# Dilated mixer: merge factors one visit later, merge two visits later, held-back output projection spread over the last visit's turns

## The chip, the core and the metric

One Trainium2 chip, one core of it. The metric is the device time of one execution in microseconds (us); the median of three runs counts. An engine is named as in the profile: PE is TensorE (matmuls), PEld its weight loads, DVE is VectorE, ACT ScalarE, POOL GpSimd and SP SyncE. SP issues the weight loads, ACT and POOL issue other DMAs.

## The reference

An encoder of two post-norm layers on 512 tokens of width 1024. Layer 0 mixes tokens by differential attention, layer 1 by dilated attention; each layer then attends into 256 memory tokens and applies a gated MLP with a convolution. Each sub-layer is `x <- LayerNorm(ALPHA * x + sublayer(x))`. The change lies in layer 1's mixer: three groups of dilated window attention, merged by their softmax denominators:

```python
qkv = (x @ w_qkv).reshape(B, S, G, 3, H, E)
for g, (window, dilation) in enumerate(((128, 1), (512, 4), (2048, 16))):
    o, l = dilated_group(qkv[:, :, g, 0], qkv[:, :, g, 1], qkv[:, :, g, 2], window, dilation, slopes)
    outs.append(o); lses.append(l)
wts = jax.nn.softmax(jnp.stack(lses), axis=0)
o = jnp.sum(wts[..., None] * jnp.stack(outs), axis=0)
return o.reshape(B, S, D) @ w_o
```

## The kernel before

All matmuls of weights are done in three passes (`mm3`, L239 to L241): an operand is split into a high and a low part (`whi`, `wlo`), and high times high, high times low and low times high are summed. SP loads a unit of weights of 512 KB into `raw` (four buffers), ACT casts the high part (L218), DVE subtracts for the low part (L219); there are six buffers for each part, and a cast waits until PE has finished with the unit that held its buffer.

The order of PE's instructions is the order in which the code issues them (`tc.manual_schedule(engines={PE})`). DVE, ACT, POOL and SP get theirs from the framework's scheduler, which plans with estimates of its own and may put an instruction ahead of one that the code issues earlier. Each engine then executes strictly in that order.

The dilated mixer (`dil_attention`) treats 16 heads as eight pairs p, and each pair in two halves v. `main` makes one visit i for each half (p = i // 2, v = i % 2), and one visit more. In visit i:

- `scores(p, v)`: 24 matmuls (L716) into four banks `S`; then for each bank and group the minimum and the bias on DVE (L725, writes `u` and the statistics `st`) and the exponential on ACT (L727). `u` has four buffers, so a bank's softmax waits for the transposes of the same bank of the visit before.
- four turns: `turn(u, n)` transposes one `u` of the visit before into a bank `t` of pool `pt`, which has two (L770), and copies it to SBUF as `PT`: DVE for n = 0 and 2, ACT for 1 and 3 (L772).
- `values` of the visit before (L785), copied into the tiles `O` (L789 to L793).

At the end of `scores(p, 1)` the code calls `factors(p)`: the statistics go to DRAM (three DMAs, `sd`) and come back in another order (`x`), all issued by POOL; DVE and ACT work out the weights of the merge (L750 to L759); they go to DRAM (`fd`) and come back broadcast as `F` (L764). At the end of `values(p, 1)` DVE merges: L795 to L797, then `evac` splits the result into `o1h` (ACT) and `o1l` (DVE), the input of the output projection.

`weave` fills the gaps in PE's order: with the next pair's projections (`proj`), and in the last three visits with the output projection of token block q = 0 (`on_.early(0)`, 12 `mm3` into `ps_a`) for the units u = 0 to 2, which use only pairs 0 to 5. The same for q = 1 is held back (`late`, 12 `mm3` into banks `S`) and taken in the last visit.

After the mixer, `OutNorm.finish` loads gain and bias of the norm (two DMAs on ACT's queue, L366, 512 KB each) and the residual rows of the four token blocks (four DMAs there, L371, 512 KB each). It computes what needs no pair 6 or 7 of blocks 2 and 3 (`first`), then the rest block by block; unit (u, hf) is the u-th of four weight units of output half hf, and unit 3 needs pairs 6 and 7. Each block is normed (`norm`: L414, L417 on DVE; L418 on ACT; L421, L422 on DVE; a power on POOL, L423; L426 on DVE), and transposed for the next sub-layer (`turn` of `OutNorm`, L432) when PE's planned time has passed a due time. The first keys of the cross-attention (`mem_keys`) are filled in behind.

Of the kernel before, what the change touches and what calls it, by code (L numbers as in the profile page):

```python
# [9 lines left out]
F32 = mybir.dt.float32  # L10
# [7 lines left out]
SEQ = 512  # L18
# [129 lines left out]
def encoder(ctx: ExitStack, tc: tile.TileContext, wall, xin, lam, subln, conv, lngb, tabf, tabd, eye, out):  # L148
# [497 lines left out]
    def dil_attention(act, oT, pools, vp, ap, on_, led):  # L646
        tab = vp.tile([128, 768], F32, name="tabd")
        nc.scalar.dma_start(tab, tabd)
        NP = LH // 2
        qk, v0, v12, st0, st12, O = {}, {}, {}, {}, {}, {}  # L650


        def keys(x, b):
# [50 lines left out]
        def scores(p, v):  # L704
            (q0, k0, q1, k1, q2, k2) = qk[p]
            if v == 0:
                st0[p] = ap.tile([128, 4, 4], F32, tag="st0", name="st0")
                st12[p] = ap.tile([128, 4, 4], F32, tag="st12", name="st12")
            bs = 2 * v, 2 * v + 1
            Ss = {(b, c): psS.tile([128, 512], F32, tag="s", name="S") for b in bs for c in range(2)}  # L710
            for b in bs:
                for q_, k_, f in ((q0, keys(k0, b), slice(0, 256)), (q1, k1[:, b, :], slice(256, 384)),
                                  (q2, k2[:, b, :], slice(384, 512))):
                    for c in range(2):
                        h = sl(c, 64)
                        nc.tensor.matmul(Ss[b, c][:, f], q_[h, b, :], k_[h], start=True, stop=True)  # L716
            us = []
            for (b, c), S in Ss.items():
                u = ap.tile([128, 512], F32, tag="u", name="u", bufs=4)
                slope = 2.0 ** (-(2 * p + c + 1) / 2.0)  # L720
                for n, s in enumerate((st0[p], st12[p])):
                    f = sl(n, 256)
                    t = tab[:, 512:768] if n else tab[:, sl(b // 3, 256)]
                    m = s[:, b, 2 * c:2 * c + 1]
                    nc.vector.tensor_tensor_reduce(out=u[:, f], in0=S[:, f], in1=t, scale=-slope,  # L725
                                                   scalar=3.0e38, op0=ALU.add, op1=ALU.min, accum_out=m)
                    nc.scalar.activation(u[:, f], u[:, f], AF.Exp, bias=m, scale=-1.0,  # L727
                                         accum_out=s[:, b, 2 * c + 1:2 * c + 2])
                us.append(u)
            if v == 1:  # L730
                O[p] = [ap.tile([128, 512], F32, tag=f"O{n}", name="O", bufs=1) for n in range(2)], factors(p)
            return us

        def factors(p):

            eng = nc.gpsimd
            sd = dram.tile([SEQ, 4], F32, name=f"sd{p}")
            fd = dram.tile([2, 2, SEQ], F32, name=f"fd{p}")
            a, b = st0.pop(p), st12.pop(p)
            eng.dma_start(sd[64:448, :].rearrange("(b p) k -> p b k", p=128), a[:, 0:3, :])  # L740
            eng.dma_start(sd[448:512, :], a[0:64, 3, :])
            eng.dma_start(sd[0:64, :], a[64:128, 3, :])
            x = ap.tile([128, 4, 4], F32, tag="x0", name="x0")
            eng.dma_start(x, sd.rearrange("(k r) c -> k r c", r=4))

            ms = [t.rearrange("p r (c k) -> p k c r", k=2) for t in (x, b)]
            w = ap.tile([128, 2, 2, 4], F32, tag="w0", name="w0")
# [14 lines left out]
            for c in range(2):  # L762
                f = fd[c]
                eng.dma_start(F[sl(c, 64)], bass.AP(f.tensor, f.offset, [[0, 64], [SEQ, 2], [1, SEQ]]))  # L764
            return F

        def turn(u, n):
            tp = bank(pt, "t").rearrange("p (a b) -> p a b", b=128)
# [6 lines left out]
        def values(p, v, PTs):  # L775
            o = bank(pt, "t")
            for x in range(2):
                b = 2 * v + x
                for n in range(4):
                    for c in range(2):  # L780
                        if n < 2:
                            V = v0[p // 2][b + n if b < 3 else 3 * n][:, (p % 2) * 128 + c * 64:]
                        else:
                            V = v12[p // 2][b][:, (p % 2) * 256 + (n - 2) * 128 + c * 64:]
                        nc.tensor.matmul(o[sl(c, 64), sl(2 * (n // 2) + x)], V[:, :64], PTs[2 * x + c][:, n, :],  # L785
                                         start=n % 2 == 0, stop=n % 2 == 1)
            (o0, o12), F = O[p]
            if v == 0:
                nc.scalar.copy(o0[:, 64:320], o[:, 0:256])  # L789
            else:  # L790
                nc.scalar.copy(o0[:, 320:512], o[:, 0:192])
                nc.scalar.copy(o0[:, 0:64], o[:, 192:256])
            nc.vector.tensor_copy(classes(o12)[:, sl(v, 2), :], o[:, 256:512].rearrange("p (r k) -> p r k", r=2))  # L793
            if v == 1:
                nc.vector.tensor_tensor(o0, o0, F[:, 0], op=ALU.mult)  # L795
                nc.vector.tensor_tensor(o12, o12, F[:, 1], op=ALU.mult)
                nc.vector.tensor_tensor(o0, o0, o12, op=ALU.add)  # L797
                evac(o0, oT[0][:, p, :], oT[1][:, p, :])

        def two_banks():  # L800
            return [psS.tile([128, 512], F32, tag="s", name="S") for _ in range(2)]
# [3 lines left out]
        def main():  # L805
            n = 2 * NP
            us = {}
            for i in range(n + 1):
                seg, step = (i // 2, 1 / 2.0) if i < n - 2 else (NP - 1, 1 / 3.0)
                pos = seg + (i - 2 * seg) * step  # L810
                yield pos
                if i < n:
                    us[i] = scores(i // 2, i % 2)
                else:
                    take(late, 1300)
                if i > 0:
                    PTs = []
                    for k in range(4):
                        yield pos + (TURN0 + TURNS * k) * step
                        PTs.append(turn(us[i - 1][k], k))  # L820
                    yield pos + VALUES * step
                    if i == n:
                        take(late, 1300)
                    values((i - 1) // 2, (i - 1) % 2, PTs)

        run(proj(0))
        weave(main(), [(proj(p + 1), 6 * 5184 + 31104 * (p % 2)) for p in range(NP - 1)]
# [124 lines left out]
    for l in range(2):  # L952
# [4 lines left out]
        with ExitStack() as cz:  # L957
# [20 lines left out]
            else:  # L978
                with ExitStack() as cp:
# [5 lines left out]
                    with ExitStack() as c:  # L985
# [2 lines left out]
                        two, pt = dil_attention(act, oT, pools, vp, ap, on, led)  # L988
                    kv = memory()
                    act, res, _ = on.finish(lambda q: two() if q == 2 else [bank(pt, "t") for _ in range(2)],  # L990
                                            [(((0, 0), (1, 0)), (2, 3))], res, False,
                                            lambda q: two if q else (pa, "a"),
                                            lambda a: mem_keys(mt_kv["mt"], kv, range(3)))
                pz = cz.enter_context(others("pz1"))
# [67 lines left out]
```

## Time and profile before

| | |
|---|---|
| three runs | 1899.86, 1897.64, 1900.0 us; median 1899.86 |
| profiled execution | 1899.72 us, of it 1897.9 us span |
| granted TensorE clock, mean | 0.998 |
| busy: PE, PEld, DVE, ACT, POOL | 1871.9, 1574.6, 952.9, 763.3, 73.0 us |
| visits of the dilated mixer | from 874.8 (first L716) to 1323 us |
| its output projection and norm | from 1323 to 1369.6 us (last L432) |

The profile lists, for each engine, the time it sat idle before an instruction and what ended that wait. `PE ps_t L770 <- DVE PT L772: 5.3, 2, 4.4` means that PE stood 5.3 us in two waits ahead of the transposes of line 770, the longest 4.4, until DVE's copy of line 772 had ended. A row of a timeline gives start, duration, engine, line, operation, output and input, count, and in brackets the wait ahead. Waits on PE cost time; waits on the others do so only if PE then waits for them.

### The profile page before, as it was taken

The numbers are of one execution on the slowest core, as the hardware profiler recorded it, in microseconds if no ns is written. First come the engines' busy times: TensorE is split into PE (matmuls) and PEld (weight loads), VectorE is DVE, ScalarE is ACT, GpSimd is POOL, SyncE is SP. The second block draws the span as 40 slices with busy tenths as digits, with TensorE's granted clock in tenths as the row PEclk, the third lists the DMA queues.
The fourth block names the chain that finished last, engine by engine and source line by source line (L and its number), as shares of the span: only waits on it lengthen the run. The fifth ranks groups of instructions, "written<-read, shape, count | busy, mean of one in ns | idle before, by whom it ended". The sixth has DMA issues, their size and how long they took to land.

```text
span 1897.9 us, 25004 instructions
## 1 busy us (share of the span) xinstructions
PE 1871.9 (99%) x9896; PEld 1574.6 (83%) x9896; DVE 952.9 (50%) x1761; ACT 763.3 (40%) x1372; POOL 73.0 (4%) x116
## 2 busy tenths in 40 slices
PE   9999999999999999999999999998999999999998
PEld 7777788889888888898898898987888898888886
DVE  5588675557444432533444344444855564444324
ACT  4567654325333321324434344343544243333211
POOL 0001110000000000000000000001000000000000
PEclk9999999999999999999999999999999999999999
DMA  6121066234332334332322232221651352333241
GB/s 237 45 78 56 23 219 191 67 118 150 100 97 93 100 100 151 104 120 100 97 77 84 78 101 87 80 80 46 224 189 65 122 157 90 99 100 96 93 144 45
DMA packets 61573, 204.35 MB, mean 108 GB/s; under 512 B 8080, under 2 KB 8720, under 8 KB 61456
## 3 DMA queue, kind: packets, MB, share of 16 engines
q1 hardware_dynamic: 46080, 165.89, 27.5%
q10 hardware_dynamic: 12816, 32.47, 4.7%
q0 software_dynamic: 2560, 4.39, 1.0%
q8 instruction: 78, 1.28, 0.3%
q14 instruction: 39, 0.32, 0.1%
HBM read 190.01 MB, written 12.71 MB: 107 GB/s over the span
## 4 chain that ended last, share of the span: by engine, by line
PE 92%; DVE 4%; DMA 2%; ACT 1%; issue 1%; POOL 0%; DVEq 0%; POOLq 0%; ACTq 0%; SPq 0%
PE ps_a L239 17%; PE ps_a L240 16%; PE ps_a L241 16%; PE ps_o L239 7%; PE ps_o L241 7%; PE ps_o L240 7%; PE ps_s L241 2%; PE ps_s L240 2%; PE ps_s L239 2%; PE ps_t L239 2%; PE ps_t L241 2%; PE ps_t L240 2%; PE S L716 1%; PE ps_t L785 1%; PE ps_t L770 1%; PE ps_o L582 1%
## 5 line engine op out<-in xcount | busy, mean ns | idle before, releaser
L219 DVE TENSOR_TENSOR wlo<-raw,whi 128x1024 fp32r<-128x1024 f32 (+1 forms) x309 | 376.7, 1220 | 454.5 <-ACT whi L218 449.3
L218 ACT CAST whi<-raw 128x1024 fp32r<-128x1024 f32 (+1 forms) x309 | 323.6, 1049 | 574.3 <-PE ps_a L240 277.6
L239 PE MATMUL ps_a<-x2h,whi 128*128 128x512 f32 (+1 forms) x384 | 152.4, 397 | 0.0
L241 PE MATMUL ps_a<-x2h,wlo 128*128 128x512 f32 (+1 forms) x384 | 146.6, 382 | 0.0
L240 PE MATMUL ps_a<-x2l,whi 128*128 128x512 f32 (+1 forms) x384 | 146.2, 381 | 0.0
L239 PE MATMUL ps_a<-whi,x2h 128*128 128x512 f32 (+1 forms) x256 | 90.2, 352 | 0.0
L725 DVE CUSTOM_DVE_ANT_0 u<-S,tabd 128x256 f32<-128x256 f32 x128 | 48.8, 420 | 79.0 <-PE ps_t L770 78.2
L240 PE MATMUL ps_a<-wlo,x2h 128*128 128x512 f32 (+1 forms) x256 | 87.1, 340 | 0.0
L241 PE MATMUL ps_a<-whi,x2l 128*128 128x512 f32 (+1 forms) x256 | 87.1, 340 | 0.0
L241 PEld LDWEIGHTS ps_a<-x2h,wlo 128*128 128x128 f32 x384 | 72.2, 188 | 14.5
L239 PEld LDWEIGHTS ps_a<-x2h,whi 128*128 128x128 f32 x384 | 72.3, 188 | 14.3 <-issue 1.5
L727 ACT ACTIVATE u<-u,st 128x256 f32<-128x256 f32 x128 | 64.0, 502 | 47.2 <-DVE st L725 47.0
L240 PEld LDWEIGHTS ps_a<-x2l,whi 128*128 128x128 f32 x384 | 72.5, 189 | 11.6
L239 PE MATMUL ps_o<-x1h,whi 128*128 128x512 f32 (+1 forms) x192 | 71.6, 373 | 0.0
L239 PE MATMUL ps_o<-x4h,whi 128*128 128x512 f32 (+1 forms) x192 | 71.6, 373 | 0.0
L240 PE MATMUL ps_a<-x4l,whi 128*128 128x512 f32 (+1 forms) x192 | 71.3, 372 | 0.0
L239 PE MATMUL ps_a<-x1h,whi 128*128 128x512 f32 (+1 forms) x192 | 71.3, 372 | 0.0
L240 PE MATMUL ps_a<-x1l,whi 128*128 128x512 f32 (+1 forms) x192 | 71.3, 372 | 0.0
L239 PE MATMUL ps_a<-x4h,whi 128*128 128x512 f32 (+1 forms) x192 | 71.3, 371 | 0.0
L241 PE MATMUL ps_a<-x4h,wlo 128*128 128x512 f32 (+1 forms) x192 | 71.3, 371 | 0.0
L241 PE MATMUL ps_a<-x1h,wlo 128*128 128x512 f32 (+1 forms) x192 | 71.3, 371 | 0.0
L241 PE MATMUL ps_o<-x1h,wlo 128*128 128x512 f32 (+1 forms) x192 | 71.3, 371 | 0.0
(420 smaller groups left out, 4487.5 us busy)
## 6 DMA issues: line engine op xcount, KB each, us to landing
raw<-in_wall_dram SPq DMA_DIRECT2D x314, 512.0 KB, 3.5
y<-row ACTq DMA_DIRECT2D x40, 256.0 KB, 3.0
row<-y ACTq DMA_DIRECT2D x20, 512.0 KB, 5.4
row<-in_lngb_dram ACTq DMA_DIRECT2D x12, 512.0 KB, 4.6
F<-fd POOLq DMA_DIRECT2D x16, 256.0 KB, 4.3
row<-in_x_dram ACTq DMA_DIRECT2D x4, 512.0 KB, 6.5
out_dram<-row ACTq DMA_DIRECT2D x8, 256.0 KB, 2.1
raw<-in_wall_dram ACTq DMA_DIRECT2D x2, 256.0 KB, 4.4
```

Of the source, the lines that this page charges most:

```text
L218: nc.scalar.copy(hi, ps)
L219: nc.vector.tensor_tensor(lo, ps, hi.bitcast(F32), op=ALU.subtract)
L239: nc.tensor.matmul(ps, ah, bh, start=start, stop=False)
L240: nc.tensor.matmul(ps, ah, bl, start=False, stop=False)
L241: nc.tensor.matmul(ps, al, bh, start=False, stop=stop)
L582: nc.tensor.matmul(o, PT[:, k, :], V[:, k, sl(h)], start=k == 0, stop=k == 3)
L716: nc.tensor.matmul(Ss[b, c][:, f], q_[h, b, :], k_[h], start=True, stop=True)
L725: nc.vector.tensor_tensor_reduce(out=u[:, f], in0=S[:, f], in1=t, scale=-slope, scalar=3.0e38, op0=ALU.add, op1=ALU.min, accum_out=m)
L727: nc.scalar.activation(u[:, f], u[:, f], AF.Exp, bias=m, scale=-1.0, accum_out=s[:, b, 2 * c + 1:2 * c + 2])
L770: nc.tensor.transpose(tp[:, k, :], u[:, sl(k)], ident)
L785: nc.tensor.matmul(o[sl(c, 64), sl(2 * (n // 2) + x)], V[:, :64], PTs[2 * x + c][:, n, :], start=n % 2 == 0, stop=n % 2 == 1)
```

## The change

`factors` is cut in two. Its DMAs to `sd` and back to `x` become `exchange(p)`, called where `factors` was, at the end of `scores(p, 1)`. The rest stays `factors(p)` and is called one visit later, after the four turns and ahead of `values`. The merge leaves `values` and becomes `merge(p)`, called in the second visit after `scores(p, 1)`, behind its second turn; the last pair's after the loop. In the last visit the held-back projection is taken three `mm3` at a time ahead of each of the four turns, where three stood ahead of the turns, three ahead of `values` and six after it. In `finish`, unit (2, 0) joins `first`, so blocks 2 and 3 compute four `mm3` more ahead of the first unit that needs pairs 6 and 7.

```diff
@@ scores @@
             if v == 1:
-                O[p] = [ap.tile([128, 512], F32, tag=f"O{n}", name="O", bufs=1) for n in range(2)], factors(p)
+                exchange(p)
             return us
-        def factors(p):
+        def exchange(p):
...
             x = ap.tile([128, 4, 4], F32, tag="x0", name="x0")
             eng.dma_start(x, sd.rearrange("(k r) c -> k r c", r=4))
+            X[p] = x
+
+        def factors(p):
+            eng = nc.gpsimd
+            fd = dram.tile([2, 2, SEQ], F32, name=f"fd{p}")
+            x, b = X.pop(p), st12.pop(p)
...
-            return F
+            Fs[p] = F
@@ values @@
-            (o0, o12), F = O[p]
+            if v == 0:
+                O[p] = [ap.tile([128, 512], F32, tag=f"O{n}", name="O", bufs=1) for n in range(2)]
+            o0, o12 = O[p]
...
-            if v == 1:
-                nc.vector.tensor_tensor(o0, o0, F[:, 0], op=ALU.mult)
-                nc.vector.tensor_tensor(o12, o12, F[:, 1], op=ALU.mult)
-                nc.vector.tensor_tensor(o0, o0, o12, op=ALU.add)
-                evac(o0, oT[0][:, p, :], oT[1][:, p, :])
+
+        def merge(p):
+            (o0, o12), F = O.pop(p), Fs.pop(p)
+            nc.vector.tensor_tensor(o0, o0, F[:, 0], op=ALU.mult)
+            nc.vector.tensor_tensor(o12, o12, F[:, 1], op=ALU.mult)
+            nc.vector.tensor_tensor(o0, o0, o12, op=ALU.add)
+            evac(o0, oT[0][:, p, :], oT[1][:, p, :])
@@ main @@
-                else:
-                    take(late, 1300)
                 if i > 0:
                     PTs = []
                     for k in range(4):
                         yield pos + (TURN0 + TURNS * k) * step
+                        if i == n:
+                            take(late, (1900, 1300)[k > 0])
                         PTs.append(turn(us[i - 1][k], k))
+                        if k == 1 and i % 2 and i > 1:
+                            merge((i - 3) // 2)
+                    if i % 2 == 0:
+                        factors((i - 2) // 2)
                     yield pos + VALUES * step
                     if i == n:
                         take(late, 1300)
                     values((i - 1) // 2, (i - 1) % 2, PTs)
+            merge(NP - 1)
@@ finish of the dilated mixer @@
-                                            [(((0, 0), (1, 0)), (2, 3))], res, False,
+                                            [(((0, 0), (1, 0), (2, 0)), (2, 3))], res, False,
```

What the scheduler makes of it is seen in the order of the built programs. DVE, in visit 14, where pair 6's factors meet the softmax (L725) and the first turn's copy of that visit; `w` are the factors, `x` what came back from DRAM. Before:

```order
L793 COPY O<-ps_t 128x2x128
L750 TENSOR_TENSOR w_10608<-x_10604,st_10368 128x8
L752 TENSOR_TENSOR w_10606<-w_10608,x_10604 128x2x4
...
L757 RECIPROCAL w_10608<-w_10608 128x8
L759 TENSOR_TENSOR w_10606<-w_10607,w_10608 128x2x4 x2
L725 ISA u,st_10754<-S,tabd 128x256
...
L772 COPY PT<-ps_t 128x512
```

And DVE at the same place in the changed program (L756 is the old L750, L778 the old L772):

```order
L801 COPY O<-ps_t 128x2x128
L756 TENSOR_TENSOR w_10831<-x_10596,st_10350 128x8
L758 TENSOR_TENSOR w_10829<-w_10831,x_10596 128x2x4
...
L763 RECIPROCAL w_10831<-w_10831 128x8
L765 TENSOR_TENSOR w_10829<-w_10830,w_10831 128x2x4 x2
L725 ISA u,st_10736<-S,tabd 128x256
...
L778 COPY PT<-ps_t 128x512
```

Nothing moved: though the code now issues the factors after visit 14's softmax and turns, the scheduler puts them ahead of both, as it did before. The same holds for every merge up to pair 6 and for ACT and POOL: up to visit 15 the four orders are the same row for row, but for line numbers and buffer names.

PE, in the last visit, from the first turn on; `S` is the held-back projection of block 1, `ps_a` that of block 0. Before:

```order
L770 MATMUL ps_t<-ident,u 128x128 x4
L239 MATMUL ps_a<-whi_10796,o1h 128x512
L240 MATMUL ps_a<-wlo_10797,o1h 128x512
L241 MATMUL ps_a<-whi_10796,o1l 128x512
L770 MATMUL ps_t<-ident,u 128x128 x4
L239 MATMUL ps_a<-whi_10822,o1h 128x512
```

And PE there in the changed program:

```order
L776 MATMUL ps_t<-ident,u 128x128 x4
L239 MATMUL ps_a<-whi_10778,o1h 128x512
L240 MATMUL ps_a<-wlo_10779,o1h 128x512
L241 MATMUL ps_a<-whi_10778,o1l 128x512
L239 MATMUL S<-whi_10523,o1h 128x512
L240 MATMUL S<-wlo_10524,o1h 128x512
...
L776 MATMUL ps_t<-ident,u 128x128 x4
```

Three `mm3` of block 1 now stand between two turns; as many fewer stand after the values.

ACT, at the start of `finish`: the cast of the last pair's merged output (`o1h`), the casts of the units (3, 0) and (3, 1) and the DMAs of gain and bias (L366) and of the residual rows (L371). Before:

```order
L218 CAST o1h<-O 128x512
L366 DMA row_11124<-in_lngb_dram 128x1024
L218 CAST whi_10935<-raw_10933 128x1024
L366 DMA row_11125<-in_lngb_dram 128x1024
L218 CAST whi_10961<-raw_10959 128x1024
L371 DMA row_11128<-y_5882 128x1024
```

And ACT there in the changed program:

```order
L218 CAST whi_10910<-raw_10908 128x1024
L218 CAST o1h<-O 128x512
L218 CAST whi_10941<-raw_10939 128x1024
L366 DMA row_11124<-in_lngb_dram 128x1024
L366 DMA row_11125<-in_lngb_dram 128x1024
L371 DMA row_11128<-y_5882 128x1024
```

Both casts of weights now stand ahead of the two DMAs of gain and bias, and these stand directly ahead of the residual rows.

More of the change, by code (lines that the diff above doesn't have):

```diff
@@ L649, in dil_attention @@
         NP = LH // 2
-        qk, v0, v12, st0, st12, O = {}, {}, {}, {}, {}, {}
+        qk, v0, v12, st0, st12, O, X, Fs = {}, {}, {}, {}, {}, {}, {}, {}
         def keys(x, b):
@@ L730, in scores @@
             if v == 1:
-                O[p] = [ap.tile([128, 512], F32, tag=f"O{n}", name="O", bufs=1) for n in range(2)], factors(p)
+                exchange(p)
             return us
-        def factors(p):
+        def exchange(p):
             eng = nc.gpsimd
             sd = dram.tile([SEQ, 4], F32, name=f"sd{p}")
-            fd = dram.tile([2, 2, SEQ], F32, name=f"fd{p}")
-            a, b = st0.pop(p), st12.pop(p)
+            a = st0.pop(p)
             eng.dma_start(sd[64:448, :].rearrange("(b p) k -> p b k", p=128), a[:, 0:3, :])
```

## The prediction

> **What bounds the kernel now.** I read the page first, then PE's waits, then the timelines of the engines around each wait. The page's head:
>
> ```profile
> span 1897.9 us, 25004 instructions
> PE 1871.9 (99%) x9896; PEld 1574.6 (83%) x9896; DVE 952.9 (50%) x1761; ACT 763.3 (40%) x1372; POOL 73.0 (4%) x116
> ```
>
> PE is idle for 26 us in all, so only PE's waits can be won. The waits from 1256 to 1350 us, the end of the mixer:
>
> ```profile
> PE ps_t L770 <- DVE PT L772: 5.3, 2, 4.4
> PE ps_a L432 <- DVE row L426: 2.1, 1, 2.1
> PE ps_t L785 <- DVE PT L772: 0.4, 1, 0.4
> ```
>
> From 860 to 1256 us, the visits 0 to 12, the same view is empty: there the factors and merges hold up nobody, and moving them is worth nothing. Two places remain. The first is visit 14 (PE, then DVE):
>
> ```profile
> 1296.00 0.63 PE L770 MATMUL ps_t<-ident,u 128*128 128x128 f32 x4 [4.37 <-DVE PT L772]
> ...
> 1307.31 0.63 PE L770 MATMUL ps_t<-ident,u 128*128 128x128 f32 x4 [0.92 <-DVE PT L772]
> ...
> 1309.50 1.97 PE L785 MATMUL ps_t<-PT,V 128*64 128x128 f32 x32 [0.43 <-DVE PT L772]
> ```
>
> ```profile
> 1292.86 0.17 DVE L750 TENSOR_TENSOR w<-x,st 128x8 f32<-128x8 f32 x1 [5.22 <-DMA x<-sd]
> ...
> 1295.17 0.68 DVE L772 COPY PT<-ps_t 128x512 f32<-128x512 f32 x1
> ...
> 1302.42 0.69 DVE L795 TENSOR_TENSOR O<-O,F 128x512 f32<-128x512 f32 x1
> ...
> 1306.47 0.69 DVE L772 COPY PT<-ps_t 128x512 f32<-128x512 f32 x1
> ```
>
> DVE stands 5.22 us at the factors of pair 6 until the statistics are back from DRAM. Behind them in its queue are the softmax and the copy that frees a bank for PE's third transpose; PE waits 4.37 us. One visit on, DVE merges pair 6 ahead of the softmax and the copy; PE waits 0.92 and 0.43 us. After the long wait PE also ran slower (stretch, busy PE, PEld, DVE, ACT and POOL, then the granted clock):
>
> ```profile
> 1291.60:1296.00 4.40, 0.03 (x1) 0.03 (x1) 2.72 (x15) 1.22 (x6) 0.76 (x1) 1.00 0.00 0
> 1296.00:1298.30 2.30, 2.30 (x11) 1.73 (x11) 1.92 (x9) 2.30 (x9) 0.36 (x1) 0.70 0.09 4
> 1298.30:1301.20 2.90, 2.90 (x35) 2.67 (x34) 0.78 (x4) 1.79 (x7) 0.71 (x2) 0.65 0.61 178
> 1301.20:1303.10 1.90, 1.90 (x26) 1.74 (x24) 1.30 (x3) 0.43 (x2) 0.00 (x0) 1.00 0.02 4
> ```
>
> At 0.70 and 0.65 of the clock 2.3 x 0.30 + 2.9 x 0.35 = 1.7 us are lost. The place is worth 4.37 + 0.92 + 0.43 + 1.7 = 7.4 us.
>
> The second place is the norm after the projection (PE, then DVE):
>
> ```profile
> 1345.95 0.66 PE L432 MATMUL ps_a<-ident,row 128*128 128x128 f32 x4 [2.14 <-DVE row L426]
> ...
> 1368.31 1.33 PE L432 MATMUL S<-ident,row 128*128 128x128 f32 x8 [0.72 <-PE ps_a L241]
> ```
>
> ```profile
> 1338.56 0.69 DVE L414 SCALAR_TENSOR_TENSOR row<-row,ps_a 128x512 f32<-128x512 f32 x1 [4.24 <-DMA row<-y]
> ...
> 1341.09 0.69 DVE L414 SCALAR_TENSOR_TENSOR row<-row,S 128x512 f32<-128x512 f32 x1 [0.98 <-DMA row<-y]
> ...
> 1345.14 1.42 DVE L426 SCALAR_TENSOR_TENSOR row<-row,sm,row 128x512 f32<-128x512 f32 x2 [0.62 <-POOL sm L423]
> ...
> 1363.58 0.42 DVE L219 TENSOR_TENSOR kv<-ps_a,kv 128x256 fp32r<-128x256 f32 x1 [0.59 <-ACT kv L218]
> ...
> 1367.46 1.40 DVE L426 SCALAR_TENSOR_TENSOR row<-row,sm,row 128x512 f32<-128x512 f32 x2
> ```
>
> The norms start when the residual rows have landed, and from then on DVE hardly rests: 17.72 of 18.00 us in the last row of the next fence. The 0.72 us ahead of the last transposes is put down to PE, but those need the norm of 1367.46. So from 1341 to 1368 us DVE sets the time, and it is started by the second residual row. DMA there (the last two columns are the share of the DMA engines and GB/s):
>
> ```profile
> 1329.00:1331.00 2.00, 2.00 (x11) 1.65 (x10) 0.93 (x3) 1.65 (x2) 0.00 (x0) 1.00 0.28 53
> 1331.00:1336.00 5.00, 5.00 (x23) 3.83 (x22) 2.34 (x2) 1.05 (x1) 0.00 (x0) 1.00 1.01 348
> 1336.00:1341.00 5.00, 5.00 (x24) 4.14 (x23) 1.52 (x5) 0.80 (x1) 0.00 (x0) 1.00 1.02 415
> 1341.00:1343.00 2.00, 2.00 (x11) 1.65 (x10) 1.91 (x4) 2.00 (x4) 0.00 (x0) 1.00 0.33 133
> ...
> 1345.00:1363.00 18.00, 17.05 (x104) 15.11 (x105) 17.72 (x30) 10.39 (x14) 2.06 (x3) 1.00 0.53 178
> ```
>
> The DMA engines are full from 1331 to 1341: six norm and residual loads and two weight units, 8 x 0.52 = 4.2 MB.
>
> **The change, part by part.**
>
> Factors a visit later: 0. In the changed program's order for DVE the factors of pair 6 still stand ahead of visit 14's softmax and copies. The DMAs that bring `x` back stand at the same place in POOL's order and are ready at the same time, since the softmax before them is unmoved. DVE therefore waits the same 5.22 us, PE the same 4.37, and the clock loses its 1.7 as before. Bounds: 0 and -6.1.
>
> Merge two visits later: 0. DVE's merge of pair 6 still stands between the copy of `O` and visit 15's softmax; 0.92 and 0.43 remain. Bounds: 0 and -1.35.
>
> Held-back projection between the turns: 0. No wait of PE in the last visit is over 0.1 us, so there is nothing to cover; six `mm3` only change place with the values. What it touches is the last pair's merge. The values end six `mm3` later, and PE needs the last pair 4 `mm3` later than before. The merge ended with `o1l`:
>
> ```profile
> 1329.87 0.69 DVE L219 TENSOR_TENSOR o1l<-O,o1h 128x512 fp32r<-128x512 f32 x1 [0.74 <-ACT o1h L218]
> ...
> 1330.89 1.23 DVE L219 TENSOR_TENSOR wlo<-raw,whi 128x1024 fp32r<-128x1024 f32 x1 [0.33 <-ACT whi L218]
> ```
>
> It ended at 1330.6, and now the weight split of 1.23 us and its cast of about 1 us go ahead of it: some 1332.3. PE, whose rows bear on this and on the next part (the first two are 12 matmuls apart, the third is the first use of the last pair, the fourth the last matmul ahead of the first transposes of the norm):
>
> ```profile
> 1326.37 0.39 PE L239 MATMUL S<-whi,o1h 128*128 128x512 f32 x1
> ...
> 1329.09 0.39 PE L239 MATMUL S<-whi,o1h 128*128 128x512 f32 x1
> ...
> 1332.74 0.39 PE L239 MATMUL ps_a<-whi,o1h 128*128 128x512 f32 x1
> ...
> 1343.42 0.39 PE L241 MATMUL S<-whi,o1l 128*128 128x512 f32 x1
> ```
>
> The first use was at 1332.74 and comes four `mm3` later, that is 12 matmuls or 2.72 us: 1335.4. The cover is 3 us; without it each us late would cost one.
>
> Unit (2, 0) drawn ahead: these four `mm3` now stand ahead of the first norm. PE reaches the first transposes at 1343.8 + 2.7 = 1346.5 instead of 1343.8, which alone would swallow their wait of 2.14 us. But no work is removed, and the transposes wait for DVE.
>
> What ACT's new order does to the DMAs, by its timeline of before:
>
> ```profile
> 1329.21 0.62 ACT L218 CAST o1h<-O 128x512 fp32r<-128x512 f32 x1 [6.50 <-DVE O L797]
> 1329.37 0.34 ACTq L366 DMA_DIRECT2D row<-in_lngb_dram  x1
> ...
> 1332.01 1.05 ACT L218 CAST whi<-raw 128x1024 fp32r<-128x1024 f32 x1 [1.15 <-PE ps_t L241]
> 1332.02 1.82 ACTq L371 DMA_DIRECT2D row<-y  x4
> ```
>
> Gain and bias were issued from 1329.37 on, the residual rows at 1332.02 behind the cast of unit (3, 1), which waits until PE has done with the buffer's old unit, (1, 0). PE reaches that point at the same time as before (what precedes it is the same set of instructions). Now gain and bias stand behind that cast too: 1332.02 - 1329.37 = 2.65 us later, and the rows behind them on the same queue, while the DMA engines are full. If the queue is worked off in order, the second row lands 2.65 us later; if only the bytes counted, a load of 0.52 MB at 415 GB/s is 1.3 us, and about one load had moved before 1332: 1.0 to 1.3. I take 2.4, near the first, as the share of the DMA engines is at its limit and one unit of weights gets its turn 0.5 us earlier.
>
> The norms start 2.4 us later, and as DVE has 0.28 us of rest in 18, the shift reaches the last transposes. On the way, small moves in the orders of ACT and DVE: a split of keys (`kv`, 0.42 us) and one of the next input (0.69, the shape of `o1l`) come ahead of the last norm; a weight split (1.2) is drawn ahead. I put -0.2 on these, between -0.8 and 1.1. PE has to wait at the transposes in any case.
>
> Sum, against the profiled execution: 1899.72 + 2.4 - 0.2 = 1901.9 us. The median lies 0.14 above that execution: 1902.0 us. A difference of 0.2%, 3.8 us, is about what a measurement of this kernel can tell from none.
>
> **The rivals.**
>
> A, slower: the clock falls once more. The wait at the last transposes grows: PE gains nothing there, and of the added 2.2 us and the 2.14 + 0.72 of before, some 3 us may fall on that one gap. After 4.37 us of idle the clock fell (rows above); after 2.14 it did not:
>
> ```profile
> 1343.80:1346.00 2.20, 0.06 (x2) 0.06 (x1) 1.58 (x6) 0.00 (x0) 0.56 (x1) 1.00 0.00 0
> 1346.00:1349.00 3.00, 3.00 (x18) 2.56 (x19) 3.00 (x5) 2.04 (x4) 0.00 (x0) 1.00 0.47 175
> ```
>
> So the point from which it decides lies between 2.2 and 4.4 us of idle PE. Price: the same 1.7 us, so 1903.7; with DVE's upper bounds, 2.65 + 1.1, it is 1905.2. Against it: the gap may be split over three transposes. Chance 0.21. [...]
>
> B, within the bound: the rows land as early as before, because the queue isn't worked off in order. Then the norms start with PE, at 1339, and PE's two waits shrink at most by 2.14 + 0.72 = 2.9 us: 1897.0. For it: weight loads on SP's queue went on at the same time. Against it: the share of the DMA engines of 1.01 and 1.02. Chance 0.14.
>
> C, faster: the change does what its code says, and the factors and merges leave DVE's queue free: -7.4 us, 1892.5. Against it stands DVE's order in the built program. Chance 0.05.
>
> **How the numbers follow.** The forecast itself has 0.60. The range goes from 1898.2 (the lower shift of 1.0 with the orders at -0.8 gives 1900.1; 1.7 less, if PE's clock happens not to fall after the wait in visit 14, gives 1898.4) to 1905.2, rival A with its bounds. Left out are C and the lower part of B, and what exceeds A. Faster by over 0.2%, under 1896.1: C, 0.05. Slower, over 1903.7: A's 0.21. The rest, 0.74, is within 0.2%.
>
> **What would show it.** Right: PE's wait of about 4.4 us at visit 14's third transpose and DVE's of about 5.2 us at L756 stand as before; gain and bias are issued at about 1332; DVE's first L414 starts near 1341 instead of 1338.6, and the last L432 near 1370.5 instead of 1368.3. Wrong: the wait in visit 14 is gone or halved (C); DVE's first L414 starts at 1339 (B); the clock falls after 1365 (A); or PE waits where I saw cover, at the last pair's `o1l`.

## The result, and the profile after

| | before | after |
|---|---|---|
| median (range) of the runs | 1898.92 us (1896.01 to 1902.91) | 1902.19 us (1899.94 to 1904.52) |
| ratio of the runs | | 1.0016, 95% interval 1.001 to 1.0023 |
| profiled execution, of it span | 1899.72, 1897.9 us | 1901.71, 1899.9 us |
| mixer's start (first L716), values of visit 15 | 874.8, 1309.50 us | 874.6, 1309.33 us |
| start of the last L432 | 1368.31 us | 1370.47 us |

The changed kernel is slower by 0.16%, 3.0 us with an interval of 1.9 to 4.4. The two profiles differ by 2.0 us, and the table says where: nothing up to visit 15, 2.2 us up to the last transposes of the norm, nothing behind them. The head of the page and PE's waits from 1256 to 1400 us (in all, times, longest):

```profile
span 1899.9 us, 25003 instructions
...
PE 1873.8 (99%) x9896; PEld 1576.5 (83%) x9896; DVE 953.5 (50%) x1761; ACT 764.0 (40%) x1372; POOL 73.0 (4%) x116
```

```profile
PE ps_t L776 <- DVE PT L778: 4.5, 2, 3.8
PE S L432 <- issue: 2.0, 1, 2.0
PE ps_a L432 <- DVE row L426: 1.4, 1, 1.4
PE ps_a L241 <- DVE wlo L219: 1.0, 1, 1.0
PE S L432 <- DVE row L426: 0.6, 1, 0.6
PE ps_t L791 <- DVE PT L778: 0.4, 1, 0.4
PE ps_o L239 <- DVE kv L219: 0.2, 1, 0.2
```

The wait of visit 14 stands (L776 is the old L770). DVE, in the same place:

```profile
1292.14 0.17 DVE L756 TENSOR_TENSOR w<-x,st 128x8 f32<-128x8 f32 x1 [4.63 <-DMA x<-sd]
```

DVE still stands at the factors until the statistics are back, with the softmax and the copy behind it. So the move that the code reads like has not taken place. The clock behind PE's wait, and the DMA engines at the start of the norm (granted clock, DMA share, GB/s are the last three columns):

```profile
1296.00:1298.30 2.30, 2.30 (x9) 1.72 (x7) 1.38 (x5) 1.93 (x8) 1.06 (x2) 0.50 0.00 0
1298.30:1301.20 2.90, 2.90 (x34) 2.61 (x32) 0.78 (x4) 1.57 (x5) 0.00 (x1) 0.66 0.65 181
1331.00:1336.00 5.00, 5.00 (x24) 4.14 (x23) 2.28 (x3) 1.05 (x1) 0.00 (x0) 1.00 0.64 186
1336.00:1341.00 5.00, 5.00 (x24) 4.14 (x23) 0.00 (x0) 0.00 (x0) 0.00 (x0) 1.00 1.02 406
1341.00:1343.00 2.00, 2.00 (x11) 1.65 (x9) 1.83 (x6) 0.23 (x1) 0.00 (x0) 1.00 1.03 416
```

From 1331 to 1336 the DMA engines carried 186 GB/s; before it was 348. The loads start later, as ACT's timeline shows:

```profile
1331.86 1.05 ACT L218 CAST whi<-raw 128x1024 fp32r<-128x1024 f32 x1 [1.15 <-PE ps_t L241]
1332.00 0.82 ACTq L366 DMA_DIRECT2D row<-in_lngb_dram  x2
1333.02 2.13 ACTq L371 DMA_DIRECT2D row<-y  x4
```

And what waits for them, on DVE and then on PE:

```profile
1341.13 0.69 DVE L414 SCALAR_TENSOR_TENSOR row<-row,ps_a 128x512 f32<-128x512 f32 x1 [6.95 <-DMA row<-y]
...
1342.66 0.69 DVE L414 SCALAR_TENSOR_TENSOR row<-row,S 128x512 f32<-128x512 f32 x1
```

```profile
1347.52 0.66 PE L432 MATMUL ps_a<-ident,row 128*128 128x128 f32 x4 [1.41 <-DVE row L426]
1363.26 0.66 PE L432 MATMUL S<-ident,row 128*128 128x128 f32 x4 [0.58 <-DVE row L426]
1365.18 0.39 PE L241 MATMUL ps_a<-mh,wlo 128*128 128x256 f32 x1 [1.03 <-DVE wlo L219]
1370.47 1.33 PE L432 MATMUL S<-ident,row 128*128 128x128 f32 x8 [1.99 <-issue]
```

The first L414 starts 2.57 us later than before (1338.56), the first transposes 1.57 later (1345.95), the last 2.16 later (1368.31). Behind the last wait the clock fell again:

```profile
1372.00:1374.00 2.00, 2.00 (x12) 2.00 (x11) 2.00 (x4) 1.39 (x2) 0.00 (x0) 0.50 0.92 319
1374.00:1376.00 2.00, 2.00 (x14) 2.00 (x13) 1.63 (x2) 0.09 (x1) 0.00 (x0) 0.65 0.72 239
```

### The profile page after: what moved, and what is told of

The parts are those of the page before. It is cut to its first block, busy times and chain, and to the rows that moved or that the text cites. A ratio compares the mean times of both kernels' runs of the same rounds, so it can differ in the third digit from the quotient of the medians.

```text
span 1899.9 us, 25003 instructions
## 1 busy us (share of the span) xinstructions
PE 1873.8 (99%) x9896; PEld 1576.5 (83%) x9896; DVE 953.5 (50%) x1761; ACT 764.0 (40%) x1372; POOL 73.0 (4%) x116
## 4 chain that ended last, share of the span: by engine, by line
PE 92%; DVE 3%; DMA 2%; ACT 1%; issue 1%; POOL 0%; ACTq 0%; DVEq 0%; POOLq 0%; SPq 0%
PE ps_a L239 17%; PE ps_a L241 17%; PE ps_a L240 17%; PE ps_o L239 7%; PE ps_o L241 7%; PE ps_o L240 7%; PE ps_s L241 2%; PE ps_s L240 2%; PE ps_s L239 2%; PE ps_t L239 2%; PE ps_t L241 2%; PE ps_t L240 2%; PE ps_t L791 2%; PE S L716 1%; PE ps_t L776 1%; PE ps_o L582 1%
## 5 line engine op out<-in xcount | busy, mean ns | idle before, releaser
L725 DVE CUSTOM_DVE_ANT_0 u<-S,tabd 128x256 f32<-128x256 f32 x128 | 48.8, 421 | 79.2 <-PE ps_t L776 78.5
```

## The experiments

Theory: the cost is the late issue of the norm's loads on ACT's queue, and the gain is missing because DVE's order did not move. Rivals: the late spread (the held-back projection spread over the last visit's turns), the unit (2, 0) or a fall of the clock costs by itself. Twelve kernels were timed, each against the kernel before on the same chip. They ran in three groups: `e_merge_only`, `e_unit_only`, `e_late_only` and `e_gb_pool`; `e_before_order`, `e_before_order_gb`, `e_order` and `e_order_gb`; and the other four. The changed kernel was timed by itself against before. Kernels of different groups can be compared only by their ratios, and such a comparison has the noise of both. The table splits their profiled executions at two points of PE's timeline: the mixer's start and the values of visit 15.

| kernel | ratio to before, 95% interval | start | visit 15's values | span | start to values | values to end |
|---|---|---|---|---|---|---|
| before | | 874.8 | 1309.50 | 1897.9 | 434.7 | 588.4 |
| after | 1.0016, 1.001 to 1.0023 | 874.6 | 1309.33 | 1899.9 | 434.7 | 590.6 |
| e_merge_only | 1.0002, 0.9993 to 1.0011 | 873.3 | 1308.12 | 1896.6 | 434.8 | 588.5 |
| e_unit_only | 1.0005, 0.9996 to 1.0015 | 874.2 | 1308.17 | 1894.6 | 434.0 | 586.4 |
| e_late_only | 1.0039, 1.0026 to 1.0051 | 876.3 | 1311.29 | 1902.2 | 435.0 | 590.9 |
| e_late_gb | 1.0028, 1.0016 to 1.0039 | 875.4 | 1310.49 | 1899.3 | 435.1 | 588.8 |
| e_gb_pool | 1.0018, 1.0009 to 1.0027 | 876.3 | 1310.57 | 1898.2 | 434.3 | 587.6 |
| e_fill | 1.0033, 1.0021 to 1.0046 | 876.1 | 1312.12 | 1902.6 | 436.0 | 590.5 |
| e_before_order | 0.9974, 0.9963 to 0.9985 | 874.2 | 1302.14 | 1888.1 | 427.9 | 586.0 |
| e_before_order_gb | 0.9971, 0.996 to 0.9982 | 875.4 | 1303.38 | 1890.2 | 428.0 | 586.8 |
| e_order_late | 1.0001, 0.9992 to 1.001 | 875.3 | 1303.23 | 1894.2 | 427.9 | 591.0 |
| e_order | 1.0008, 0.9999 to 1.0016 | 874.5 | 1302.47 | 1894.8 | 428.0 | 592.3 |
| e_order_gb | 0.9984, 0.9975 to 0.9992 | 873.8 | 1301.75 | 1891.9 | 428.0 | 590.2 |
| e_order_gb_fill | 0.9987, 0.9978 to 0.9996 | 875.1 | 1303.08 | 1893.1 | 428.0 | 590.0 |

The start lies between 873.3 and 876.3 us though no kernel differs ahead of it, and the kernel before was profiled in one of its longer executions (1899.72 us, its medians in these comparisons 1896.59 to 1898.92). So a single profile's total is good to about 3 us only; costs are read from the ratios, places from the stages.

### One part alone

**The factors and merges alone** (`e_merge_only`): `exchange`, the later `factors` and `merge` of the change, the rest as before.

> The kernel before with the factors one visit later and the merge two visits later, and nothing else of the change. Theory: the scheduler issues the same rows in the same order on PE, DVE and ACT as before, so PE's wait of 3.8 to 4.4 us in visit 14 stays and the time is that of before within the spread of the runs (1 us). Rival (the move does what its code says): PE's wait in visit 14 goes and the kernel takes 5 to 7 us less; rival of the cost: the moved merge makes the 3 us that the whole change cost.

The ratio of 1.0002 (0.9993 to 1.0011) says no change, its stages are those of before (434.8 and 588.5 us against 434.7 and 588.4), and PE's waits in visits 14 and 15 are still there:

```profile
1293.96 1.08 PE L776 MATMUL ps_t<-ident,u 128*128 128x128 f32 x4 [3.79 <-DVE PT L778]
1305.92 0.63 PE L776 MATMUL ps_t<-ident,u 128*128 128x128 f32 x4 [0.73 <-DVE PT L778]
1308.12 1.97 PE L791 MATMUL ps_t<-PT,V 128*64 128x128 f32 x32 [0.43 <-DVE PT L778]
```

This part of the change alters the source, and on the chip nothing.

**The unit (2, 0) alone** (`e_unit_only`):

```diff
-                                            [(((0, 0), (1, 0)), (2, 3))], res, False,
+                                            [(((0, 0), (1, 0), (2, 0)), (2, 3))], res, False,
```

> The kernel before with one edit alone: unit (2, 0) of blocks 2 and 3 drawn ahead of the first norm. ACT's order of casts and loads stays as before. Theory (late loads): gain and bias issued near 1329.4, first L414 near 1338.6 to 1339.0, PE's first wait at L432 falls from 2.14 to under 0.5 us but the last L432 stays within 0.7 us of 1368.3, and the time within 1 us of before. Rival (this unit is the cost): the last L432 near 1370.5 and 2 to 3 us more than before.

1.0005 (0.9996 to 1.0015): it costs nothing that can be told, and PE's wait of 2.14 us at the first transposes is gone (no wait stands behind the row):

```profile
1344.77 0.60 PE L432 MATMUL ps_a<-ident,row 128*128 128x128 f32 x4
```

The rival that the unit costs falls. The last transposes start at 1365.44 us, earlier than the 1368.3 expected, but that gain of this one profile is not in the timings.

**The late spread alone** (`e_late_only`):

```diff
-                else:
-                    take(late, 1300)
...
+                        if i == n:
+                            take(late, (1900, 1300)[k > 0])
```

> The kernel before with one edit alone: the held-back projection spread over the last visit's turns. In its program order both weight casts stand ahead of the gain and bias loads on ACT, as in the changed kernel. Theory (late loads): gain and bias are issued near 1332 instead of 1329.4, the first L414 starts near 1341 instead of 1338.6, the last L432 near 1370 to 1370.5, and the kernel takes 2 to 4 us more than before. Rival (the unit drawn ahead of the first norm delays the norms): this kernel leaves that unit where it was, so the last L432 stays near 1368.3 and the time within 0.5 us of before.

1.0039 (1.0026 to 1.0051), 7.4 us: more than the whole change, and more than the 2 to 4 us expected. Its profiled stage behind the values is 2.5 us longer than before's (590.9 against 588.4); the rest of the 7.4 is not located. ACT has the changed kernel's order, with both casts ahead of gain and bias; PE's wait at the first transposes, and the clock behind it:

```profile
1333.93 0.82 ACTq L366 DMA_DIRECT2D row<-in_lngb_dram  x2
```

```profile
1349.49 0.86 PE L432 MATMUL ps_a<-ident,row 128*128 128x128 f32 x4 [4.17 <-DVE row L426]
```

```profile
1349.50:1352.00 2.50, 2.50 (x10) 2.10 (x11) 2.50 (x5) 0.59 (x1) 0.00 (x0) 0.56 0.56 209
1352.00:1354.00 2.00, 2.00 (x9) 1.67 (x8) 1.83 (x3) 1.48 (x2) 0.00 (x0) 0.70 0.01 1
```

In the changed kernel, which draws unit (2, 0) ahead as well, this wait is 1.41 us and the clock holds there (1.00 from 1348 to 1350). So the spread is the costly part; that the unit's four `mm3` (2.7 us) repair part of it is read from these two kernels.

### The loads taken off ACT's queue

One line, in the changed kernel (`e_gb_pool`) and in the one with the late spread alone (`e_late_gb`):

```diff
-                    nc.scalar.dma_start(gb[n], bass.AP(lngb.tensor, lngb.offset + (ln * 2 + n) * D,
+                    (nc.gpsimd if ln == 3 else nc.scalar).dma_start(gb[n], bass.AP(lngb.tensor, lngb.offset + (ln * 2 + n) * D,
```

> The changed kernel with gain and bias of this one norm loaded from POOL's queue instead of ACT's, behind the last F load. Theory (late loads): gain and bias are issued before 1330, the residual rows land 2 us earlier or more, the first L414 starts near 1339 when PE has ended block 0, the last L432 near 1368, and the time falls by 2 to 4 us against the changed kernel, to within 1.5 us of before. Rival (the order of PE's and DVE's work is the cost, not the loads): the last L432 stays near 1370.5 and the time 2 to 4 us above before.

> The kernel before with the late spread alone, and gain and bias of this norm issued by POOL. The late spread alone cost 0.0039, with PE's wait at the first transposes at 4.17 us and a fall of the clock behind it, and ACT's order had put two casts ahead of gain and bias. Theory (the late spread costs by way of ACT's order, which delays the loads, and by nothing else): the wait at the first transposes is 2 us or less, the clock does not fall there, and the ratio is 1.000 to 1.001. Rival (the spread costs by itself, through the place of the matmuls in the last visit and the later merge of the last pair): the ratio stays at 1.003 or above, with waits of PE between the values and the first transposes.

The rows came earlier, the time did not follow. In `e_gb_pool` the rows land earlier (DVE), and PE no longer waits at the first transposes:

```profile
1337.55 0.69 DVE L414 SCALAR_TENSOR_TENSOR row<-row,ps_a 128x512 f32<-128x512 f32 x1 [2.13 <-DMA row<-y]
```

From visit 15's values to the last transposes it is 57.8 us, where after had 61.1 and before 58.8. The ratio is 1.0018 (1.0009 to 1.0027) all the same, where 1.0016 (1.001 to 1.0023) stood: the theory had the last transposes right (1368.38 us), the rival the time. In `e_late_gb` the 4.17 us and the fall of the clock at the first transposes are gone (1.00 from 1340 to 1368); the ratio is 1.0028 (1.0016 to 1.0039) against 1.0039 (1.0026 to 1.0051), and neither theory's numbers are met: the time is above the one's 1.001, and the waits between values and transposes that the other asks for are not there. Both kernels wait longer at the last transposes instead, with a fall of the clock behind (0.51 and 0.50 from 1370 to 1372), `e_gb_pool` first, then `e_late_gb`:

```profile
1368.38 0.93 PE L432 MATMUL S<-ident,row 128*128 128x128 f32 x4 [2.38 <-issue]
```

```profile
1369.40 0.85 PE L432 MATMUL S<-ident,row 128*128 128x128 f32 x4 [2.76 <-issue]
```

Their stages behind the values, 587.6 and 588.8 us, are about as long as before's 588.4, so the 3.4 and 5.3 us of their ratios are not located by these profiles. For the changed kernel this leaves the theory of the late loads unproven: its profile shows the delay and the path by which it reaches the last transposes, but the timings show nothing won when the delay is taken away.

### DVE's order forced

The factors are tied behind DVE's copy of the visit's third turn, and the merge is called at the fourth turn behind the same copy. In the changed kernel this is `e_order`; with the line above, `e_order_gb`; in the kernel before with only the factors and merges moved, `e_before_order` and `e_before_order_gb`.

```diff
-            (nc.scalar.copy if n % 2 else nc.vector.tensor_copy)(PT, tp)
+            cp = (nc.scalar.copy if n % 2 else nc.vector.tensor_copy)(PT, tp)
+            if n % 2 == 0:
+                state["cp"] = cp.ins
...
-                        if k == 1 and i % 2 and i > 1:
-                            merge((i - 3) // 2)
+                        if k == 3 and i % 2 and i > 1:
+                            with tc.issue_after(state["cp"]):
+                                merge((i - 3) // 2)
...
-                        factors((i - 2) // 2)
+                        with tc.issue_after(state["cp"]):
+                            factors((i - 2) // 2)
```

> The kernel before with the factors and the merge moved as in the change, and DVE's order forced (both behind DVE's copy of the third turn); the held-back projection and the units drawn ahead stay as before. Theory: the 7.4 us of visits 14 and 15 (4.37 + 0.92 + 0.43 of waits and 1.7 of clock) go and nothing else moves but one cast on ACT, which now stands ahead of gain and bias: -7.4 + (0 to 1.3), a ratio of 0.9961 to 0.9968. Rival (a wait that is removed in the mixer comes back at the norm, since DVE and the loads set the time there): PE's wait at the first transposes grows from 2.1 by the 4 to 7 us won, and the ratio is 0.999 to 1.000.

> As the run before, with gain and bias of this norm issued by POOL. Theory: the loads then lie ahead of the projection's end, the first norm starts when PE has its sum, and of the 2.14 and 0.72 us of waits at the norm some 1 to 2 us go too: a ratio of 0.9952 to 0.9963, faster than both kernels. Rival (as in the run on the changed kernel, the earlier loads give nothing, since the order of ACT and DVE in the last norm moves): within 0.0007 of the run before.

> The changed kernel, with DVE's order forced to be what the code of the change reads like: the factors stand behind DVE's copy of the visit's third turn, and the merge of an odd visit is called at the fourth turn and stands behind the same copy. Theory (the change gains nothing in visits 14 and 15 because the scheduler leaves the factors and the merge ahead of the softmax and the copies): the waits of 3.80, 0.73 and 0.43 us and the 1.7 to 2.3 us that the clock loses behind the first of them go, 6 to 7 us. Part of it is given back: on ACT three casts of weights now stand ahead of gain and bias instead of two, so the norms of the output projection start 0 to 2.7 us later than in the changed kernel. Sum against the kernel before: +3.2 - 6.5 + (0 to 2.7), that is a ratio of 0.998 to 1.000. Rival (the long wait comes from something else than DVE's queue, such as the exponentials on ACT or the buffers of u): a wait of 3 to 4 us stands there still, and the ratio is 1.0016 or above.

> As the run before (factors and merge forced behind DVE's copies), and gain and bias of this norm issued by POOL instead of ACT. Theory: both losses go, the 6 to 7 us of visits 14 and 15 and what the late loads cost; but the run with POOL's issue alone stayed 0.0018 above the kernel before, so from that one only the first can be counted on: +3.4 - 6.5 is -3 us, a ratio of 0.998; with the late loads' 2.4 us it is 0.997. Rival (the place on ACT's queue costs nothing by itself, it is the order of the last norm that costs): the same time as the run before within 1 us, and the last transposes wait 2 us as there.

`e_before_order` shows what visits 14 and 15 are worth. PE's waits from 1256 to 1400 us are all that is left of the list:

```profile
PE ps_t L793 <- DVE PT L778: 0.9, 2, 0.4
PE ps_a L432 <- DVE row L426: 0.7, 1, 0.7
PE ps_a L239 <- DVE kv L219: 0.5, 1, 0.5
PE ps_o L239 <- DVE kv L219: 0.2, 1, 0.2
```

DVE's factors now stand behind the copy and wait for nothing:

```profile
1292.22 0.69 DVE L778 COPY PT<-ps_t 128x512 f32<-128x512 f32 x1
1293.51 0.17 DVE L756 TENSOR_TENSOR w<-x,st 128x8 f32<-128x8 f32 x1
```

From the mixer's start to the values of visit 15 it takes 427.9 us where it was 434.0 to 436.0 in the eight kernels with DVE's old order. The whole is 0.9974 (0.9963 to 0.9985), 4.9 us faster with an interval of 2.8 to 7.0; the 6.1 to 7.4 us expected lie at its upper end and just beyond. The rival, that the gain comes back as a wait at the norm, falls for this kernel (0.7 us there). Taking the loads to POOL adds nothing to it: 0.9971 (0.996 to 0.9982); gain and bias were not late in it (issued 20.3 us behind the values of visit 15, before 19.9). The 0.9952 to 0.9963 expected were missed, as the rival said. Both are faster than both kernels of the case.

`e_order` has the same 428.0 us up to visit 15, and is nevertheless no faster than before: 1.0008 (0.9999 to 1.0016), above the 0.998 to 1.000 expected. The rival (another cause of the long wait) falls, since that wait is gone. Its ACT rows and PE's first transposes:

```profile
1328.09 1.05 ACT L218 CAST whi<-raw 128x1024 fp32r<-128x1024 f32 x1 [0.88 <-DMA raw<-in_wall_dram]
1328.24 0.82 ACTq L366 DMA_DIRECT2D row<-in_lngb_dram  x2
```

```profile
1343.66 0.66 PE L432 MATMUL ps_a<-ident,row 128*128 128x128 f32 x4 [4.44 <-DVE row L426]
...
1366.30 1.34 PE L432 MATMUL S<-ident,row 128*128 128x128 f32 x8 [2.02 <-issue]
```

Gain and bias are issued 25.8 us behind the values of visit 15 (1328.24 - 1302.47) where it was 19.9 before and 22.7 after: a third cast of weights stands ahead of them, and it waits for its weights. PE waits 4.44 us at the first transposes. With the loads from POOL the same kernel is 0.9984 (0.9975 to 0.9992), 4.6 us less, and the intervals don't touch; the first wait is 0.5. Here, where the loads are latest, their place on ACT's queue is shown to cost. `e_order_gb` still lies above `e_before_order_gb`, though these intervals overlap; its profile has a wait of 3.06 us at the last transposes, with the clock at 0.50 from 1361 to 1367 us.

**The spread put into the forced order** (`e_order_late`: `e_before_order` and the spread, no unit):

> The kernel before with factors and merge moved and forced behind DVE's copies, and the late spread; the units drawn ahead stay as before. With the unit (2, 0) drawn ahead as well the ratio was 1.0008, without the spread and the unit 0.9974. Theory (the spread, through ACT's order, is what gives the gain of visits 14 and 15 back): with casts ahead of gain and bias and no unit to fill PE's wait, PE waits 4 us or more at the first transposes, the clock falls there, and the ratio is 1.000 to 1.002. Rival (the unit drawn ahead gives it back, because it takes work from behind the norms): a ratio of 0.997 to 0.998.

1.0001 (0.9992 to 1.001) against 0.9974: the spread takes the whole gain back, 5.1 us, and the trace agrees (values to end 591.0 against 586.0). From 1256 to 1400 us PE waits 7.5 us in all, in `e_before_order` 2.3; the difference of 5.2 is as large as the loss. The 4 us and the fall of the clock that were expected at the first transposes did not come. PE's waits show three places. The last pair's `o1h` now stands behind two casts on ACT and PE waits for it, and the norm's transposes wait as well; the clock holds at 1.00 behind each:

```profile
1328.05 0.50 PE L239 MATMUL ps_a<-whi,o1h 128*128 128x512 f32 x1 [1.64 <-ACT o1h L218]
...
1342.27 0.66 PE L432 MATMUL ps_a<-ident,row 128*128 128x128 f32 x4 [2.48 <-DVE row L426]
...
1365.02 1.34 PE L432 MATMUL S<-ident,row 128*128 128x128 f32 x8 [0.96 <-PE ps_a L241]
```

### The fall of the clock at the last transposes

Eight transposes of the identity, 1.3 us of PE, ahead of the last block's, in the changed kernel (`e_fill`) and in `e_order_gb` (`e_order_gb_fill`); their result is overwritten:

```diff
+            for k in range(8 if self.ln == 3 and q == 3 and n == 0 else 0):
+                nc.tensor.transpose(tps[:, k % 4, :], ident, ident)
```

> The changed kernel with eight more transposes of the identity on PE just ahead of the last block's transposes (1.3 us of PE; their result is overwritten). In the changed kernel's profile PE waited 1.99 us there and the clock fell to 0.50 for 3 us behind it. Theory (that fall is a loss of the size of the other, 1.7 us, and is part of the change's cost): the wait falls below 1 us, the clock stays at 1.00, and the ratio falls from 1.0016 to 1.0007. Rival (the fall costs nothing, since PE at half speed only swallows the later wait for the split of keys, which in the kernel before was 1.2 us): the clock stays at 1.00, that wait comes back, and the ratio stays within 0.0004 of 1.0016.

> The changed kernel with factors and merge forced behind DVE's copies and gain and bias issued by POOL (0.9984), and the same eight transposes ahead of the last block's. There PE waited 3.06 us and the clock was at 0.50 to 0.58 for 6 us behind it, 2.8 us lost. Theory (that loss is what separates it from the same kernel without the late spread and the unit, 0.9971): a wait of 1.8 us, no fall, a ratio of 0.9969 to 0.9975. Rival (the clock's loss is swallowed behind, and DVE's chain sets the time): 0.998 and above.

Inconclusive. The wait at the last transposes shrank as meant (0.71 and 1.09 us, the clock at 1.00 behind), but in both executions the clock fell earlier instead: in `e_order_gb_fill` behind a wait of 1.91 us at the first transposes (0.50 from 1344 to 1346), in `e_fill` behind two short waits (L434 is the old L432):

```profile
1366.11 0.66 PE L434 MATMUL S<-ident,row 128*128 128x128 f32 x4 [0.91 <-DVE row L426]
1368.03 0.39 PE L241 MATMUL ps_a<-mh,wlo 128*128 128x256 f32 x1 [1.02 <-DVE wlo L219]
```

```profile
1368.00:1370.00 2.00, 1.97 (x10) 1.97 (x11) 2.00 (x4) 1.75 (x4) 0.00 (x0) 0.57 0.53 132
```

The ratios, 1.0033 (1.0021 to 1.0046) and 0.9987 (0.9978 to 0.9996), show no gain in either kernel, and neither lies where the theory put it; that the gap at the last transposes alone carries a loss that could be won is not supported.

## Why the prediction was right, and where its steps failed

**PE's waits at two places bound this stretch.** Right for visits 14 and 15: with DVE's order changed the stage shortens by 6 to 8 us (434.0 to 436.0 against 427.9 to 428.0), where 7.4 was put. The ratio gives 4.9 (2.8 to 7.0). For the norm it is not shown that PE's waits there are worth anything: in `e_unit_only` and `e_gb_pool` the wait at the first transposes is gone, and neither is faster than before.

**Factors and merge later: 0.** Right, and for the reason given: alone they are 1.0002 (0.9993 to 1.0011), and in the changed kernel DVE stands 4.63 us at L756 (forecast about 5.2) and PE 3.80 (about 4.4).

**Spread: 0 in itself, with cover at the last pair's `o1l`.** The row was right: `o1l` ended at 1332.06 us, forecast 1332.3, and PE did not wait there:

```profile
1331.37 0.69 DVE L219 TENSOR_TENSOR o1l<-O,o1h 128x512 fp32r<-128x512 f32 x1
```

But alone the spread costs 0.39% (0.26 to 0.51), and 0.28% (0.16 to 0.39) with the loads early again. So the step that put all of its cost on the place of gain and bias in ACT's queue fails in size, and in the changed kernel taking them off that queue won nothing (1.0018). In the forced order a second place is shown, the wait for `o1h`; in the kernels with the old order the rest is not located.

**Unit (2, 0): no gain.** Right alone (1.0005, 0.9996 to 1.0015). Missed: beside the spread it is worth something. With it PE's wait at the first transposes is 1.41 us instead of 4.17, the clock does not fall there, and the ratio is 1.0016 instead of 1.0039. This holds for the old order only. In the forced order the kernel with the unit (`e_order`) is at 1.0008 (0.9999 to 1.0016) and waits 4.44 us there, the one without it (`e_order_late`) is at 1.0001 (0.9992 to 1.001) and waits 2.48; with the unit a third cast had come ahead of the loads.

**ACT's order: loads 2.65 us later, rows 2.4, order effects -0.2.** Gain and bias were issued at 1332.00 (forecast about 1332), the first L414 came at 1341.13 (near 1341), the last L432 at 1370.47 (near 1370.5). The two terms were mis-sized and cancelled. The chain was said to start with the second residual row; that one no longer waited (1342.66, no wait, against 1341.09 with 0.98), so the shift that reached the first transposes is 1.57 and not 2.4. Between them and the last transposes 0.59 were added (2.16 - 1.57) where -0.2 was put for the orders, inside its bounds.

**The sum**, 1901.9 us for the profiled execution, was 1901.71. That it came this near is in part luck: two errors of 0.8 us cancelled, and single executions of the changed kernel lie between 1899.94 and 1904.52. The median forecast, 1902.0 against 1902.19, started from a median before of 1899.86, where the 21 runs gave 1898.92; so 2.1 us were forecast and 3.0 (1.9 to 4.4) came. The lower end of the range, 1898.2, is 0.2 below its own working (1898.4).

**Rival A**, the clock: it fell in the changed kernel's profile as the rival says, behind a wait of 1.99 us, below the 2.2 from which the rival should decide. This was one of the prediction's own signs of being wrong. Yet from the last transposes to the end it took 529.4 us (1899.9 - 1370.47) and before it 529.6, so the fall cost nothing on balance there, where the rival had put 1.7. PE's later waits for the split of keys shrank, in the whole execution, from the first to the second of these rows (before, then after):

```profile
PE ps_a L239 <- DVE kv L219: 3.0, 3, 1.6
```

```profile
PE ps_a L239 <- DVE kv L219: 1.9, 2, 1.2
```

The wait of 1.25 us at 1382.43 is the one that is gone. That the one pays for the other is argued from these rows; the eight added transposes were to show it and did not.

**Rival B** (the rows land as early): refuted by the 1341.13. **Rival C** (the change does what its code says): refuted by L756, and its price was wrong as well. `e_order` does what the code says, and is at 1.0008 (0.9999 to 1.0016), because the loads come later still (with POOL's issue it is 0.9984). A gain near the 7.4 us of its price came only without the spread, and it was 4.9 (`e_before_order`).

Open: where the spread's cost lies in the old order once the loads are early, and why `e_gb_pool` is no faster than the changed kernel though its profiled stage behind the values is 3.0 us shorter.

## What to carry to other kernels

Where a scheduler orders an engine, look at the built order before believing that a move in the source took place, and force it if the move is the point: here forcing it was worth 4.9 us and the move without it nothing. A cast that moves on a queue can move a DMA issue behind it: here gain and bias came 19.9 us behind the values of visit 15, 22.7 with two casts of weights ahead of them on ACT's queue and 25.8 with three, so work that shifted such a cast shifted loads that nobody edited. Look, too, at the queues behind a wait that is removed: in the forced order the 4.9 us won were gone again with the spread (1.0001 against 0.9974), as PE's waits from 1256 to 1400 us grew from 2.3 to 7.5 us.

## What the hardware showed that was not expected

In these runs the clock's fall has no sharp threshold in the length of one wait. From 1256 us on, all waits of PE from 2.76 us up (visit 14's 3.42 to 4.79 in eight kernels, then 4.44, 4.17, 3.06, 2.76) were followed by a fall of the granted clock. Of those between 1.8 and 2.5 us it fell behind 1.91, 1.99, 2.2 (`e_merge_only`, 0.50 from 1382 to 1384) and 2.38, and held behind 1.88, 2.02, 2.14 and 2.48. It also fell behind 0.91 and 1.02 us that stood 1.9 us apart (`e_fill`, 0.57 from 1368 to 1372). The lowest granted clock in any window of a fall was 0.50, as in the row of 1296.00 to 1298.30 above. The kernel before shows 0.50 from 1297.0 to 1300.0 us, too, with 0.91 in the half microsecond ahead, 0.68 in the one behind and 1.00 outside these: the 0.70 and 0.65 that the prediction read there are windows that reach over an end of the fall.
